# Root-mean-square pooling over four neighbours in fp32 in place: stores in groups of four loads, two of them behind the last load

## The chip, the cores and the metric

The kernel runs on one core of one Trainium2 chip. The metric is the device time of one execution in microseconds (us); lower is better. The core's engines work side by side: ScalarE (ACT in the profile), VectorE (DVE), GpSimd (POOL), SyncE (SP) and TensorE (PE), the last of which is not used here. Transfers between the chip's main memory (HBM) and the core's on-chip memory (SBUF, 128 partitions) are issued from an engine's queue and carried out by 16 DMA engines.

## The reference

The input is 32 x 256 x 4096 numbers in fp32, 134.22 MB. Along the last axis every four neighbours become one number: the square root of the mean of their squares (p is 2, kernel_size is 4). The output is 32 x 256 x 1024 in fp32, 33.55 MB.

```python
for i in range(out_length):                 # out_length = 4096 // 4
    window = np.abs(x[:, :, 4 * i:4 * i + 4]) ** 2.0
    result[:, :, i] = np.mean(window, axis=-1) ** 0.5
```

## The kernel before

The first two axes are flattened to 8192 rows of 4096 numbers. A tile is 256 rows, two consecutive rows for each of the 128 partitions, so that a partition has 8192 numbers (32 KB) and a tile 4 MB; the whole tile is one contiguous stretch of HBM. There are 32 tiles, and one loop over them.

For each tile, the load `xt` (line 50) is issued from SP's queue into one of three input buffers. The tile's arithmetic goes in two halves of 4096 numbers a partition:

- ACT squares the half from `xt` into a tile `x2` in bf16 (line 60);
- DVE adds the first two of every four to the last two, with a `scalar_tensor_tensor` over 2048 pairs, into `c` in bf16 (line 66);
- DVE adds the two numbers that are left, with a second one over 1024, into `sum4` in bf16 (line 73);
- ACT takes the root, with the factor 1/4 as its scale, into half of the output tile `ot` in fp32 (line 78).

When both halves are done, the 1 MB of `ot` are stored by an issue on ACT's queue (line 84). A store's partition holds 8 KB, and there are 32 stores. The tiles `x2`, `c` and `sum4` come from a pool with four buffers each, `ot` from another with four.

The order of the instructions on each engine is set by the framework's scheduler, which also puts in the waits: a load waits until the squares have read the buffer that it is to fill; a square waits for its load, a sum for its square, a root for its sum, and a store for the roots. In the profile, names lose their numbers: `x` stands for `x2` and `sum` for `sum4`.

Of the kernel before, what the change touches and what calls it, by code (L numbers as in the profile page):

```python
# [1 line left out]

# [4 lines left out]


@with_exitstack
def kernel(  # L10
    ctx: ExitStack,
    tc: tile.TileContext,
    x: bass.AP,
    p: float,
    kernel_size: int,
    out: bass.AP,
):
    nc = tc.nc

    assert float(p) == 2.0, "kernel specialized for p == 2"  # L20
    k = int(kernel_size)
    assert k == 4, "kernel specialized for kernel_size == 4"

    x_flat = x.flatten_outer_dims()
    out_flat = out.flatten_outer_dims()
    R, L = x_flat.shape
    P = nc.NUM_PARTITIONS

    ROWS_PER_PART = 2
    CHUNK_ROWS = P * ROWS_PER_PART  # L30
    CL = L * ROWS_PER_PART
    CLo = CL // k
    assert R % CHUNK_ROWS == 0
    n_tiles = R // CHUNK_ROWS
    n_halves = 2
    HL = CL // n_halves
    HLo = HL // k

    fp32 = mybir.dt.float32
    bf16 = mybir.dt.bfloat16  # L40

    in_pool = ctx.enter_context(tc.tile_pool(name="in_pool", bufs=3))
    mid_pool = ctx.enter_context(tc.tile_pool(name="mid_pool", bufs=4))
    out_pool = ctx.enter_context(tc.tile_pool(name="out_pool", bufs=4))

    for i in range(n_tiles):
        rows = slice(i * CHUNK_ROWS, (i + 1) * CHUNK_ROWS)

        xt = in_pool.tile([P, CL], fp32)
        nc.sync.dma_start(  # L50
            out=xt,
            in_=x_flat[rows].rearrange("(p t) l -> p (t l)", t=ROWS_PER_PART),
        )

        ot = out_pool.tile([P, CLo], fp32)
        for h in range(n_halves):
            xh = xt[:, h * HL:(h + 1) * HL]

            x2 = mid_pool.tile([P, HL], bf16)
            nc.scalar.activation(  # L60
                out=x2, in_=xh, func=mybir.ActivationFunctionType.Square,
            )

            x2v = x2.rearrange("p (n j) -> p n j", j=k)
            c = mid_pool.tile([P, 2 * HLo], bf16)
            nc.vector.scalar_tensor_tensor(  # L66
                out=c.rearrange("p (n j) -> p n j", j=2),
                in0=x2v[:, :, 0:2], scalar=1.0, in1=x2v[:, :, 2:4],
                op0=mybir.AluOpType.mult, op1=mybir.AluOpType.add,
            )  # L70
            cv = c.rearrange("p (n j) -> p n j", j=2)
            sum4 = mid_pool.tile([P, HLo], bf16)
            nc.vector.scalar_tensor_tensor(  # L73
                out=sum4, in0=cv[:, :, 0], scalar=1.0, in1=cv[:, :, 1],
                op0=mybir.AluOpType.mult, op1=mybir.AluOpType.add,
            )

            nc.scalar.activation(  # L78
                out=ot[:, h * HLo:(h + 1) * HLo], in_=sum4,
                func=mybir.ActivationFunctionType.Sqrt,  # L80
                scale=1.0 / k,
            )

        nc.scalar.dma_start(
            out=out_flat[rows].rearrange("(p t) l -> p (t l)", t=ROWS_PER_PART),
            in_=ot,
        )


# [1 line left out]
_INS = ['x', 'p', 'kernel_size']  # L91
_OUTS = [((32, 256, 1024), 'float32')]
#: Inputs that are plain numbers.
_NUMBERS = {'p': 2.0, 'kernel_size': 4}


# [26 lines left out]
```

## Time and profile before

| what | value |
|---|---|
| median of 10 runs | 404.67 us (404.61 to 404.8) |
| the profiled execution's own time | 404.62 us |
| its span in the trace | 402.7 us |
| DVE busy | 224.3 us (56%), 128 operations |
| ACT busy | 293.0 us (73%) |
| load queue (q1) | 134.22 MB, 77.5% of the 16 DMA engines' span |
| store queue (q10) | 33.56 MB, 19.8% |
| mean rate over the span | 417 GB/s |

The span is the time from the first to the last event that the trace of the one core holds; the device time has 1.92 us more around it. The trace's page shows busy time of each engine, then the span in 40 slices of about 10 us with busy tenths (9 is 90% or more) and the rate of the DMA engines, then the DMA queues, and the chain of work that ended last. A row of the grouped instructions reads: line, engine, operation, output from input, shapes (partitions x elements, type), count; busy us in total, mean ns of one; idle time of the engine ahead of them, and what ended it. A row of the timeline begins with its start and its duration in us. A row of the windows begins with the stretch, then has its length, the busy time and number of instructions of DVE, ACT and POOL, TensorE's clock, the busy share of the DMA engines and the rate in GB/s. SPq and ACTq are the queues of DMA issues on SP and ACT.

### The profile page before, as it was taken

What the parts mean: (1) busy time and instruction counts of PE and PEld (TensorE: products, weight loads), DVE (VectorE), ACT (ScalarE), POOL (GpSimd) and SP (SyncE); (2) the same over time, 40 slices, a digit from 0 to 9 for tenths busy, and PEclk for the clock granted to TensorE, in tenths of its full rate; (3) what the DMA queues carried; (4) which work ended last, traced back from release to release, by engine and by line L of the source; (5) the groups of instructions that cost most, each with busy time, mean ns of one, the idle gap of its engine ahead of it and who ended that gap; (6) DMA issues with size and microseconds to landing.
All of it is one profiled execution on the core that took longest, in us unless ns stands there. A gap on an engine that the chain in (4) does not pass through costs nothing.

```text
span 402.7 us, 424 instructions
## 1 busy us (share of the span) xinstructions
DVE 224.3 (56%) x128; ACT 293.0 (73%) x130; POOL 0.2 (0%) x4
## 2 busy tenths in 40 slices
DVE  0357466645556554466544566455566554566454
ACT  1788777787676886767977677876767977677872
POOL 0000000000000000000000000000000000000000
DMA  9999999999999999999999999999999999999962
GB/s 361 420 430 403 443 446 404 439 456 404 456 415 431 443 430 426 444 409 448 439 414 445 425 429 448 429 422 444 409 448 427 421 450 425 429 448 404 439 259 104
DMA packets 9219, 167.80 MB, mean 417 GB/s; under 512 B 1024, under 2 KB 1024, under 8 KB 1024
## 3 DMA queue, kind: packets, MB, share of 16 engines
q1 hardware_dynamic: 4608, 134.22, 77.5%
q10 hardware_dynamic: 4608, 33.56, 19.8%
q14 instruction: 3, 0.02, 0.0%
HBM read 134.22 MB, written 33.55 MB: 417 GB/s over the span
## 4 chain that ended last, share of the span: by engine, by line
DMA 58%; ACT 26%; DVE 9%; issue 6%; SPq 0%; ACTq 0%
DMA xt<-in_x_dram 58%; ACT x L60 22%; DVE c L66 6%; ACT ot L78 4%; DVE sum L73 3%; SPq L50 0%; ACTq L78 0%
## 5 line engine op out<-in xcount | busy, mean ns | idle before, releaser
L60 ACT ACTIVATE x<-xt 128x4096 bf16<-128x4096 f32 x64 | 229.1, 3604 | 58.7 <-DMA xt<-in_x_dram 58.7
L66 DVE SCALAR_TENSOR_TENSOR c<-x 128x2048 bf16<-128x2048 bf16 x64 | 146.7, 2292 | 170.4 <-ACT x L60 170.4
L78 ACT ACTIVATE ot<-sum 128x1024 f32<-128x1024 bf16 x64 | 67.1, 1049 | 45.5 <-DVE sum L73 43.8
L73 DVE SCALAR_TENSOR_TENSOR sum<-c 128x1024 bf16<-128x1024 bf16 x64 | 78.4, 1225 | 2.2
L60 ACT ACT_TABLE_LOAD x1 | 1.3, 1283 | 0.7 <-PEq L104 0.7
L78 ACT ACT_TABLE_LOAD x1 | 1.3, 1283 | 0.0
L104 POOL MEMSET const-bfloat16-1.0<- 128x1 bf16 x1 | 0.1, 102 | 0.0
L104 POOL MEMSET const-uint8-127<- 128x1 uint8 x1 | 0.1, 101 | 0.0
L104 POOL MEMSET const-float32-0.0<- 128x1 f32 x1 | 0.1, 99 | 0.2 <-issue 0.2
L104 POOL MEMSET const-float32-1.0<- 128x1 f32 x1 | 0.1, 98 | 0.0
## 6 DMA issues: line engine op xcount, KB each, us to landing
xt<-in_x_dram SPq DMA_DIRECT2D x32, 4096.0 KB, 28.3
out_dram<-ot ACTq DMA_DIRECT2D x32, 1024.0 KB, 16.6
```

What stands on the lines that cost most here:

```text
L60: nc.scalar.activation(out=x2, in_=xh, func=mybir.ActivationFunctionType.Square,)
L66: nc.vector.scalar_tensor_tensor(out=c.rearrange("p (n j) -> p n j", j=2), in0=x2v[:, :, 0:2], scalar=1.0, in1=x2v[:, :, 2:4], op0=mybir.A ...
L73: nc.vector.scalar_tensor_tensor(out=sum4, in0=cv[:, :, 0], scalar=1.0, in1=cv[:, :, 1], op0=mybir.AluOpType.mult, op1=mybir.AluOpType.add,)
L78: nc.scalar.activation(out=ot[:, h * HLo:(h + 1) * HLo], in_=sum4, func=mybir.ActivationFunctionType.Sqrt, scale=1.0 / k,)
L104: nc = _bacc.Bacc("TRN2", target_bir_lowering=False, num_devices=1)
```

## The change

- The layout. The flat input is cut into 32 chunks of 128 x 8192 numbers, and the chunks into groups: seven of four chunks, one of three (chunks 28 to 30) and one of one (chunk 31). Within a group, a partition has one contiguous stretch of HBM, 128 KB in a group of four, and a chunk is a piece of 32 KB of each. So a load still brings 32 KB a partition, but the pieces of neighbouring partitions lie 128 KB apart (96 KB in the group of three, 32 KB in the last).
- The stores. One store a group instead of one a tile: nine in all, of 4 MB (32 KB a partition) for a group of four. Stores of groups 0 to 5 and of the last are issued on ACT's queue after the group's last root. Those of groups 6 and 7 (`held`) are issued on SP's queue after everything else there, that is, behind the last load.
- The arithmetic. Everything is fp32. The square is written over its input in `xt`; one `tensor_reduce` on DVE adds the four neighbours into the group's output tile; the root is taken in place there. The tiles `x2`, `c` and `sum4` are gone.
- The buffers. Four input buffers instead of three, two output buffers of 32 KB a partition, one of 8 KB for the last chunk.
- The order. It is written out by hand (`manual_schedule`). Three loads are issued ahead of the loop and load i+3 at the top of step i; the root of a half is issued on ACT after the square of the next half.
- The first load is issued from ACT's queue, the others from SP's.

The diff, its core:

```diff
-    in_pool = ctx.enter_context(tc.tile_pool(name="in_pool", bufs=3))
-    mid_pool = ctx.enter_context(tc.tile_pool(name="mid_pool", bufs=4))
-    out_pool = ctx.enter_context(tc.tile_pool(name="out_pool", bufs=4))
+    W = 8192
+    CH = 4096
+    GROUP = 4
+    LAST = 1
...
+    while i < n - LAST:
+        g = min(GROUP, n - LAST - i)
+        groups.append((i, g))
+        i += g
+    groups += [(j, 1) for j in range(n - LAST, n)]
+    held = {len(groups) - 1 - LAST - j for j in range(2)}
...
+    in_pool = ctx.enter_context(tc.tile_pool(name="in_pool", bufs=4))
+    out_pool = ctx.enter_context(tc.tile_pool(name="out_pool", bufs=2))
+    last_pool = ctx.enter_context(tc.tile_pool(name="last_pool", bufs=1))
+    ctx.enter_context(tc.manual_schedule())
...
+    def x_block(i):
+        first, g = groups[group_of[i]]
+        block = xf[first * W * P:(first + g) * W * P].rearrange("(p w) -> p w", p=P)
+        return block[:, (i - first) * W:(i - first + 1) * W]
...
+    def load(i):
+        xt = in_pool.tile([P, W], fp32)
+        queue = nc.scalar if i == 0 else nc.sync
+        queue.dma_start(out=xt, in_=x_block(i))
+        xts[i] = xt
+
+    def root(i, c):
+        first, g = groups[group_of[i]]
+        ot = ots[group_of[i]]
+        at = ((i - first) * W + c) // k
+        o = ot[:, at:at + CH // k]
+        nc.scalar.activation(
+            out=o, in_=o, func=mybir.ActivationFunctionType.Sqrt, scale=1.0 / k,
         )
+        if i == first + g - 1 and c + CH == W and group_of[i] not in held:
+            nc.scalar.dma_start(out=out_block(group_of[i]), in_=ot)
...
+    for i in range(3):
+        load(i)
+    pending = None
+    for i in range(n):
+        if i + 3 < n:
+            load(i + 3)
...
+        for c in range(0, W, CH):
+            xh = xts[i][:, c:c + CH]
             nc.scalar.activation(
-                out=x2, in_=xh, func=mybir.ActivationFunctionType.Square,
+                out=xh, in_=xh, func=mybir.ActivationFunctionType.Square,
             )
...
+            nc.vector.tensor_reduce(
+                out=ots[gi][:, at:at + CH // k],
+                in_=xh.rearrange("p (n j) -> p n j", j=k),
+                axis=mybir.AxisListType.X, op=mybir.AluOpType.add,
             )
...
+            if pending is not None:
+                root(*pending)
+            pending = (i, c)
+    root(*pending)
+    for gi in sorted(held):
+        nc.sync.dma_start(out=out_block(gi), in_=ots[gi])
```

More of the change, by code (lines that the diff above doesn't have):

```diff
@@ L22 @@
     assert k == 4, "kernel specialized for kernel_size == 4"
-    x_flat = x.flatten_outer_dims()
-    out_flat = out.flatten_outer_dims()
-    R, L = x_flat.shape
     P = nc.NUM_PARTITIONS
[L29 to L37, printed above, removed]
-    fp32 = mybir.dt.float32
-    bf16 = mybir.dt.bfloat16
-    in_pool = ctx.enter_context(tc.tile_pool(name="in_pool", bufs=3))
@@ L43 @@
-    mid_pool = ctx.enter_context(tc.tile_pool(name="mid_pool", bufs=4))
-    out_pool = ctx.enter_context(tc.tile_pool(name="out_pool", bufs=4))
[L46 to L52, printed above, removed]
-        )
[L55 to L59, printed above, removed]
+    fp32 = mybir.dt.float32
@@ new lines @@
+    xf = x.rearrange("b c l -> (b c l)")
+    of = out.rearrange("b c l -> (b c l)")
+    total = xf.shape[0] // P
+    W = 8192
+    CH = 4096
+    GROUP = 4
+    LAST = 1
+    n = total // W
+    assert n * W == total
+    groups = []
+    i = 0
+    while i < n - LAST:
[4 more added lines that the diff above has]
+    held = {len(groups) - 1 - LAST - j for j in range(2)}
+    group_of = {}
+    for gi, (first, g) in enumerate(groups):
+        for j in range(g):
+            group_of[first + j] = gi
@@ new lines, with out_block @@
+    in_pool = ctx.enter_context(tc.tile_pool(name="in_pool", bufs=4))
[6 more added lines that the diff above has]
+        return block[:, (i - first) * W:(i - first + 1) * W]
+    def out_block(gi):
+        first, g = groups[gi]
+        return of[first * W * P // k:(first + g) * W * P // k].rearrange("(p w) -> p w", p=P)
@@ new lines @@
+    xts = {}
+    ots = {}
+    def load(i):
[10 more added lines that the diff above has]
+            out=o, in_=o, func=mybir.ActivationFunctionType.Sqrt, scale=1.0 / k,
+        )
+        if i == first + g - 1 and c + CH == W and group_of[i] not in held:
+            nc.scalar.dma_start(out=out_block(group_of[i]), in_=ot)
@@ L60 @@
+    for i in range(3):
[4 more added lines that the diff above has]
+            load(i + 3)
+        gi = group_of[i]
+        first, g = groups[gi]
+        if i == first:
+            pool = last_pool if i >= n - LAST else out_pool
+            ot = pool.tile([P, g * W // k], fp32)
+            ots[gi] = ot
+        for c in range(0, W, CH):
+            xh = xts[i][:, c:c + CH]
             nc.scalar.activation(
-                out=x2, in_=xh, func=mybir.ActivationFunctionType.Square,
+                out=xh, in_=xh, func=mybir.ActivationFunctionType.Square,
@@ L62 @@
             )
[L64 to L69, printed above, removed]
-            )
[L71 to L87, printed above, removed]
+            at = ((i - first) * W + c) // k
+            nc.vector.tensor_reduce(
+                out=ots[gi][:, at:at + CH // k],
+                in_=xh.rearrange("p (n j) -> p n j", j=k),
+                axis=mybir.AxisListType.X, op=mybir.AluOpType.add,
+            )
```

## The prediction

> **What bounds the kernel now.** I read the page from the top: busy shares, slices, queues, chain.
>
> ```profile
> span 402.7 us, 424 instructions
> DVE 224.3 (56%) x128; ACT 293.0 (73%) x130; POOL 0.2 (0%) x4
> DMA  9999999999999999999999999999999999999962
> GB/s 361 420 430 403 443 446 404 439 456 404 456 415 431 443 430 426 444 409 448 439 414 445 425 429 448 429 422 444 409 448 427 421 450 425 429 448 404 439 259 104
> ...
> q1 hardware_dynamic: 4608, 134.22, 77.5%
> q10 hardware_dynamic: 4608, 33.56, 19.8%
> ...
> DMA 58%; ACT 26%; DVE 9%; issue 6%; SPq 0%; ACTq 0%
> ```
>
> No compute engine is full; the 16 DMA engines are, in 38 of 40 slices, and loads (q1) and stores (q10) together hold 97.3% of them. The chain that ended last names the DMA for 58% only, because it goes through the squares that free an input buffer; but the transfer rate doesn't sag while it does. So the kernel is bound by bytes, and what can be won lies where the DMA row is not 9: the two ends. The windows view gives these by stretch (engine busy times, clock, DMA share, GB/s):
>
> ```profile
> 5.00:385.00 380.00, 217.12 (x124) 281.58 (x124) 0.00 (x0) 1.00 1.00 431
> 0.00:1.60 1.60, 0.00 (x0) 0.88 (x1) 0.20 (x4) 1.00 0.00 0
> ...
> 385.00:390.00 5.00, 0.37 (x2) 4.74 (x3) 0.00 (x0) 1.00 0.78 321
> 390.00:398.50 8.50, 6.84 (x4) 5.44 (x3) 0.00 (x0) 1.00 0.00 1
> 398.50:402.70 4.20, 0.00 (x0) 0.00 (x0) 0.00 (x0) 1.00 0.61 250
> ...
> 401.40:401.80 0.40, 0.00 (x0) 0.00 (x0) 0.00 (x0) 1.00 0.02 0
> ```
>
> For 380 us the share is 1.00 at 431 GB/s. At the end the DMA stands still for over 8.5 us, and the timeline shows what it waits for: the last tile's arithmetic.
>
> ```profile
> 386.22 3.60 ACT L60 ACTIVATE x<-xt 128x4096 bf16<-128x4096 f32 x1
> 386.34 0.34 ACTq L84 DMA_DIRECT2D out_dram<-ot  x1
> 389.73 3.60 ACT L60 ACTIVATE x<-xt 128x4096 bf16<-128x4096 f32 x1
> ...
> 393.36 2.29 DVE L66 SCALAR_TENSOR_TENSOR c<-x 128x2048 bf16<-128x2048 bf16 x1
> ...
> 395.68 1.23 DVE L73 SCALAR_TENSOR_TENSOR sum<-c 128x1024 bf16<-128x1024 bf16 x1
> 396.94 1.06 ACT L78 ACTIVATE ot<-sum 128x1024 f32<-128x1024 bf16 x1 [2.45 <-DVE sum L73]
> 398.03 0.34 ACTq L84 DMA_DIRECT2D out_dram<-ot  x1
> ```
>
> Squares, sums and root of tile 31 run with nothing left to move; only then is its 1 MB stored.
>
> **The change, part by part.**
>
> *Held stores (the main term).* The stores of chunks 24-27 (4 MB) and 28-30 (3 MB) go onto SP's queue behind load 31. Their bytes are not new; they are moved from beside the loads to behind the last one: 7.34 MB at 431 GB/s, 17.0 us of transfer that covers the last chunk's arithmetic. Nothing is queued behind them on SP, and load 31 stands ahead of them, so no load waits for a root. What becomes free is the standstill: 0.22 x 5.00 = 1.1 us in 385-390, 8.5 us in 390-398.5, and in the last 4.2 us a 0.39 share, 1.6 us, less the 1.3 us from 401.4 to 402.7 that any last store has. Together 9.9 us; some of the 1.1 us is only the 16 engines ending unevenly, so I take 9.6, with 9.0 and 9.9 as ends.
>
> Whether the cover holds is a race, priced with these rows:
>
> ```profile
> L60 ACT ACTIVATE x<-xt 128x4096 bf16<-128x4096 f32 x64 | 229.1, 3604 | 58.7 <-DMA xt<-in_x_dram 58.7
> L66 DVE SCALAR_TENSOR_TENSOR c<-x 128x2048 bf16<-128x2048 bf16 x64 | 146.7, 2292 | 170.4 <-ACT x L60 170.4
> L78 ACT ACTIVATE ot<-sum 128x1024 f32<-128x1024 bf16 x64 | 67.1, 1049 | 45.5 <-DVE sum L73 43.8
> L73 DVE SCALAR_TENSOR_TENSOR sum<-c 128x1024 bf16<-128x1024 bf16 x64 | 78.4, 1225 | 2.2
> ```
>
> and, for the time from the last store's issue (398.03) to its bytes, the windows
>
> ```profile
> 398.40:398.80 0.40, 0.00 (x0) 0.00 (x0) 0.00 (x0) 1.00 0.00 0
> 398.80:399.20 0.40, 0.00 (x0) 0.00 (x0) 0.00 (x0) 1.00 0.98 410
> ```
>
> The new sum over four has no row. The two DVE rows give (2292-1225)/1024 = 1.04 ns a position and 158 ns fixed. A reduction that takes one input a cycle has 4096 positions: 4.43 us. If it took two inputs a cycle, as the two-operand sums do, 2.29 us; at half speed for 4-byte data, 158 + 8536 = 8.7 us. I take 4.43: nothing in the rows shows a penalty for 4-byte data (the square reads it and the root writes it: the difference of their means, 2555 ns over 3072 elements, is one 0.83 ns slope for both). By the same token square and root in fp32 stay 3.60 and 1.05.
>
> From the end of load 31's bytes, with 1.6 us until ACT sees it (an estimate, as long as from the span's start to the first packets): square 0 ends at 5.2, the held-back root of chunk 30 at 6.2, so SP, which waits for just that root, issues store 28-30 with its first bytes some 0.8 us later (398.03 to 398.80 above), at 7.0. Store 24-27, long released, lasts till 9.7: 2.7 us of slack. Square 1 ends at 9.7, reduction 0 at 9.6, reduction 1 at 14.1, the last root at 15.2, its store's bytes start at 16.0. The held stores end at 17.0: 1.0 us of slack. The last MB then ends with the rest and the 1.3 us closing follows.
>
> *Compute between the loads.*
>
> ```profile
> 360.98 1.06 ACT L78 ACTIVATE ot<-sum 128x1024 f32<-128x1024 bf16 x1 [2.67 <-DVE sum L73]
> 361.94 3.60 ACT L60 ACTIVATE x<-xt 128x4096 bf16<-128x4096 f32 x1
> ...
> 365.45 3.60 ACT L60 ACTIVATE x<-xt 128x4096 bf16<-128x4096 f32 x1
> ```
>
> By the distances of these starts a half costs ACT 3.51 for the square (361.94 to 365.45) and 0.96 for the root, 4.47 us; DVE 4.43 plus a handover of 0.03. A chunk takes 8.9 us. A load alone takes 4.19 MB / 431 = 9.7 us, and on average with its store 12.2. So compute keeps up even in stretches with loads only, by 0.8 us a chunk: no cost, the DMA covers it. If that cover went, each us a chunk beyond 9.7 delays the last six chunks first. DVE rises from 225 to 283 us, ACT stays near 297, both under 390. Four input buffers instead of three: a chunk's buffer is free some 14 us after it lands, while two to three loads are still queued, so no load starts late.
>
> *Fewer, longer stores.* 33.56 MB cost 19.8% of 402.7 = 79.7 us in 8 KB pieces a partition; at the loads' price (77.5% for 134.22 MB, 312.1 us) they would cost 78.0. The gain is up to 1.7 us. Against it: a store alone is seen once, 1.05 MB from 398.8 to 401.4, at 403 GB/s; if all 8.39 MB of the new tail ran so, they would lose 1.4 us. I take -1.5, since that lone MB holds the start and uneven end that only the last store will have.
>
> Mid-run stores will share the engines evenly with the loads. The issues by line (KB each, us to landing):
>
> ```profile
> xt<-in_x_dram SPq DMA_DIRECT2D x32, 4096.0 KB, 28.3
> out_dram<-ot ACTq DMA_DIRECT2D x32, 1024.0 KB, 16.6
> ```
>
> and the timeline's start shows what the first load moves past:
>
> ```profile
> 0.72 1.28 ACT L60 ACT_TABLE_LOAD   x1 [0.72 <-PEq L104]
> 0.73 19.64 SPq L50 DMA_DIRECT2D xt<-in_x_dram  x4
> 12.90 7.12 ACT L60 ACTIVATE x<-xt 128x4096 bf16<-128x4096 f32 x2 [10.89 <-DMA xt<-in_x_dram]
> ```
>
> 1 MB takes 16.6 us to land beside loads, far over its own 2.6, so queues alternate; with equal pieces a 4 MB store takes about 19.5 us and a load beside it twice 9.7. A group comes every 49 us and has two output buffers, so no reduction waits for a store. The 0.34 us issue on ACT falls from 32 to 7; hidden.
>
> *First load on ACT's queue.* It then shares the engines with load 1 and both land near 21 us instead of the first at 12.9. Compute starts 8-9 us later, which the 3.3 us a chunk (12.2 less 8.9) wins back; the DMA is busy with four queued loads (39 us). Cost 0; ends -0.4 (one SP issue saved) and +1.3 (the table load goes first and holds it back).
>
> **Sum**, against the profiled execution, 404.62 us = span 402.7 + 1.92 around it (median of ten runs 404.67, so nothing to correct): -9.6 - 1.5, and +0.5 for unevenness at three new queue hand-overs (a guess, between 0 and the 1.1 us that the present end shows): 394.0 us.
>
> **Rivals.** (B) *The cover tears.* The slack of 1.0 us is thin. If reductions take 4.9 us or more a half, compute falls behind 9.7 us loads by 0.1 us a chunk and up, over six chunks, and the last root comes after the held stores; likewise if landing takes longer. Each us late is a us of standstill, at most the 9.6. Middle: 398.
>
> (C) *Loads run slower in the new layout.* A partition's row is now 128 KB from the next one instead of 32 KB. Each per cent off the loads is 3.1 us; from 10.6 / 312.1 = 3.4% on the change loses. Priced by the page's slices: the slow ones near 404 GB/s against 431 would make the loads 332 us, +20, thus 414. For it: no row shows such a distance; against: 8 KB and 32 KB distances now run within 2% of one another.
> The Trainium skill, page "DMA: Bandwidth & Descriptors", section "Latency and other measured facts", says that large power-of-two distances between partitions' rows in HBM slow copies: 207 GB/s at 512 KiB against 214 at full rate, far less at megabytes. Taken at 128 KB that 3.3% would be 10.3 us, by estimate 404, no change; no trace here shows it, and a quarter of that distance should cost less.
>
> (D) *Slower: the halves wait for one another.* Square 1 now writes the very tile that reduction 0 reads, and root and reduction share one output tile. If the waits go by whole tile, a half runs in series: 3.60 + 4.43 + 1.05 = 9.1 us, 64 of them 581 us, plus ends about 600. It decides when a half exceeds 6.1 us (12.2 a chunk). Before shows no such sharing between engines; the slices written are disjoint, which speaks against it.
>
> (E) *The reduction at half speed:* 64 x 8.7 = 556, with first load and tail some 580 us. Slower than before from about 5.6 us a half on. Against: the slopes above.
>
> **How the numbers follow.** A (as summed) 0.76, B 0.12, C 0.05, D 0.04, E 0.03. A's terms at their good ends together give 392.6 (9.9, 1.7 and 0.4 off, the hand-overs at nothing), at their bad ends 399.4 (9.0 off, 1.4, 1.3 and 1.1 on); that range takes in most of B as well and leaves out some 0.15. Ten runs lie within 0.05%; I take 0.2%, 0.8 us, as what can be told from no change. Faster: A and B, 0.88. Within: the part of C with 3.2 to 3.7% off the loads and its near surroundings, 0.02. Slower: the rest of C, D and E, 0.10.
>
> **What would show it.** Right: reductions near 4.43 us; DMA share 1.00 up to 2 us before the end; three last store issues (SP, SP, ACT) whose bytes join without a gap; first square near 21 us. Wrong: a hole in the DMA row after the last load (B); q1 per byte dearer (C); squares waiting for the DVE (D, E).

## The result, and the profile after

The changed kernel takes 395.46 us (median of 8 runs, 395.25 to 395.60) against 404.68 us before: a ratio of 0.9771, 95% interval 0.9762 to 0.9779. The forecast was 394.0 us with a range of 392.6 to 399.4; its span would have been 392.1 us, and is 393.4. In all comparisons below, the kernel before ran on the same chip beside the others, at 404.61 to 404.68 us.

From the page of the changed kernel: span, busy shares, DMA slices, queues, and the two groups whose duration was forecast.

```profile
span 393.4 us, 357 instructions
DVE 282.8 (72%) x64; ACT 294.0 (75%) x130; POOL 0.2 (0%) x4
DMA  8999999999999999999999999999999999999997
...
q1 hardware_dynamic: 4752, 137.37, 81.3%
q10 hardware_dynamic: 1152, 30.41, 18.0%
...
L113 DVE TENSOR_REDUCE ot<-xt 128x1024 f32<-128x4096 f32 x64 | 282.8, 4419 | 103.1 <-ACT xt L109 102.3
L109 ACT ACTIVATE xt<-xt 128x4096 f32<-128x4096 f32 x64 | 230.8, 3608 | 87.5 <-DMA xt<-in_x_dram 85.0
```

The last two slices, 6 and 2 before, are 9 and 7. DVE works 58 us more than before and nothing becomes longer by it. The tail, by the windows (stretch, busy times, clock, DMA share, GB/s) and by the timeline:

```profile
5.00:385.00 380.00, 281.90 (x64) 291.68 (x128) 0.00 (x0) 1.00 1.00 431
385.00:390.00 5.00, 0.86 (x1) 1.06 (x1) 0.00 (x0) 1.00 0.97 372
390.00:393.40 3.40, 0.00 (x0) 0.00 (x0) 0.00 (x0) 1.00 0.46 195
```

```profile
363.63 3.62 ACT L109 ACTIVATE xt<-xt 128x4096 f32<-128x4096 f32 x1 [0.55 <-DMA xt<-in_x_dram]
...
373.34 3.62 ACT L109 ACTIVATE xt<-xt 128x4096 f32<-128x4096 f32 x1 [0.54 <-DMA xt<-in_x_dram]
...
377.93 0.34 SPq L123 DMA_DIRECT2D out_dram<-ot  x1
...
385.89 1.06 ACT L88 ACTIVATE ot<-ot 128x1024 f32<-128x1024 f32 x1 [3.39 <-DVE ot L113]
386.98 0.34 ACTq L92 DMA_DIRECT2D out_dram<-ot  x1
```

The middle runs at the same 431 GB/s as before. In 385-390 the DMA now stands still for 0.03 x 5.00 = 0.15 us and in the last 3.4 us for 0.54 x 3.40 = 1.8 us. The same sum over the tail before was 1.1 + 8.5 + 1.6 = 11.2 us. So 9.2 us of standstill went, and the span fell by 402.7 - 393.4 = 9.3 us: all of the gain lies in the tail. While the last chunk is worked, the 7 MB behind load 31 move. (The 372 GB/s in 385-390 do not mean a hole: a window counts a transfer with all its bytes where it starts, so that the long pieces under way at 385 are counted ahead of it.) The timeline's first two rows show the pace: chunks 30 and 31 begin 9.71 us apart, and each time ACT has waited about half a microsecond for the load, so compute is not behind.

Whether the held stores alone do this, and what the rest of the change is worth, the page can't tell. Twelve more kernels were run for it.

### The profile page after: what moved, and what is told of

It is laid out like the page before. It is cut to its first block, busy times and chain, and to the rows that moved or that the text cites. A ratio compares the mean times of both kernels' runs of the same rounds, so it can differ in the third digit from the quotient of the medians.

```text
span 393.4 us, 357 instructions
## 1 busy us (share of the span) xinstructions
DVE 282.8 (72%) x64; ACT 294.0 (75%) x130; POOL 0.2 (0%) x4
## 4 chain that ended last, share of the span: by engine, by line
DMA 65%; ACT 21%; DVE 11%; issue 0%; ACTq 0%
DMA xt<-in_x_dram 65%; ACT xt L109 18%; DVE ot L113 11%; ACT ot L88 3%; ACT L88 0%; ACTq L109 0%
## 5 line engine op out<-in xcount | busy, mean ns | idle before, releaser
L113 DVE TENSOR_REDUCE ot<-xt 128x1024 f32<-128x4096 f32 x64 | 282.8, 4419 | 103.1 <-ACT xt L109 102.3
L109 ACT ACTIVATE xt<-xt 128x4096 f32<-128x4096 f32 x64 | 230.8, 3608 | 87.5 <-DMA xt<-in_x_dram 85.0
L88 ACT ACTIVATE ot<-ot 128x1024 f32<-128x1024 f32 x64 | 67.0, 1047 | 4.2 <-DVE ot L113 3.4
```

Of the source, the lines that this page charges most:

```text
L88: nc.scalar.activation(out=o, in_=o, func=mybir.ActivationFunctionType.Sqrt, scale=1.0 / k,)
L109: nc.scalar.activation(out=xh, in_=xh, func=mybir.ActivationFunctionType.Square,)
L113: nc.vector.tensor_reduce(out=ots[gi][:, at:at + CH // k], in_=xh.rearrange("p (n j) -> p n j", j=k), axis=mybir.AxisListType.X, op=mybir. ...
```

## Experiments

**1. The changed kernel with nothing held.**

```diff
-    held = {len(groups) - 1 - LAST - j for j in range(2)}
+    held = set()
```

> The changed kernel with every store issued on ACT's queue after its group's last root, none held behind the last load. Theory (the held stores fill the standstill of the tail): the 4 MB of chunks 24-27 go back beside the loads, load 31 lands 9.7 us later, and only the 3 MB of chunks 28-30 and the last 1 MB are left behind it. Their bytes start about 7 us after the last load's bytes end, so a hole of some 7 us opens, a second of 1 to 2 us after them, and the time is 403.9 us (402.5 to 405). Rival (the gain comes from longer stores, the fp32 arithmetic or the order): 395.5 to 397.

Measured: 403.58 us (403.30 to 404.05), ratio 0.9972 (0.9962 to 0.9982). The windows of the tail:

```profile
380.00:385.00 5.00, 4.97 (x2) 4.43 (x3) 0.00 (x0) 1.00 0.26 111
385.00:390.00 5.00, 4.18 (x2) 4.58 (x3) 0.00 (x0) 1.00 0.37 157
390.00:395.00 5.00, 4.44 (x2) 2.66 (x2) 0.00 (x0) 1.00 0.97 418
395.00:402.00 7.00, 1.17 (x1) 1.06 (x1) 0.00 (x0) 1.00 0.46 188
```

Between 380 and 390 the DMA stands still for 3.7 + 3.2 = 6.9 us, then come the 3 MB and, after a second hole, the last one. Without the held stores 8.1 of the 9.2 us are gone. Where the remaining 1.1 us come from was not taken apart.

**2. The kernel before with the seven stores ahead of its last one held.**

```diff
-    mid_pool = ctx.enter_context(tc.tile_pool(name="mid_pool", bufs=4))
-    out_pool = ctx.enter_context(tc.tile_pool(name="out_pool", bufs=4))
+    mid_pool = ctx.enter_context(tc.tile_pool(name="mid_pool", bufs=2))
+    out_pool = ctx.enter_context(tc.tile_pool(name="out_pool", bufs=8))
...
-        nc.scalar.dma_start(
...
+        if n_tiles - 8 <= i < n_tiles - 1:
+            kept.append((to, ot))
+        else:
+            nc.scalar.dma_start(out=to, in_=ot)
+    for to, ot in kept:
+        nc.sync.dma_start(out=to, in_=ot)
```

> The kernel before with one thing changed: the stores of tiles 24 to 30 (seven of 1 MB) are issued on SP's queue behind the last load; eight output buffers instead of four, and two buffers instead of four for the bf16 tiles to make room. Theory (held stores alone carry the gain): 7.34 MB, 17 us, cover the last tile's 12 us of arithmetic; 404.68 less 8.8 is 395.9 us (395.2 to 397). Rival (the gain needs the fp32 arithmetic, the hand-written order or the longer stores): 400 to 405.

Measured: 402.40 us (402.36 to 402.44), ratio 0.9943 (0.9929 to 0.9956). The theory as it stood is wrong: this edit brings 2.3 us, not 8.8. The timeline of ACT shows why (the squares and roots are one line further down than in the kernel before):

```profile
371.03 1.06 ACT L79 ACTIVATE ot<-sum 128x1024 f32<-128x1024 bf16 x1 [2.45 <-DVE sum L74]
371.99 7.11 ACT L61 ACTIVATE x<-xt 128x4096 bf16<-128x4096 f32 x2
379.21 1.06 ACT L79 ACTIVATE ot<-sum 128x1024 f32<-128x1024 bf16 x1
382.71 1.06 ACT L79 ACTIVATE ot<-sum 128x1024 f32<-128x1024 bf16 x1 [2.45 <-DVE sum L74]
383.68 7.11 ACT L61 ACTIVATE x<-xt 128x4096 bf16<-128x4096 f32 x2
...
394.40 1.06 ACT L79 ACTIVATE ot<-sum 128x1024 f32<-128x1024 bf16 x1 [2.45 <-DVE sum L74]
395.49 0.34 ACTq L89 DMA_DIRECT2D out_dram<-ot  x1
```

```profile
385.00:390.00 5.00, 2.66 (x2) 5.00 (x2) 0.00 (x0) 1.00 0.80 338
390.00:395.00 5.00, 4.33 (x3) 2.44 (x3) 0.00 (x0) 1.00 0.00 0
395.00:400.60 5.60, 0.00 (x0) 0.46 (x1) 0.00 (x0) 1.00 0.45 187
```

From tile 25 on, both squares of a tile run first, then both of its roots, and the second root waits 2.45 us for its sums with the next tile's squares behind it. A tile begins every 383.68 - 371.99 = 11.69 us. That would be enough where a load comes with its store (12.2 us), but with the stores held a load alone takes 9.7 us. ACT falls 2 us further behind at each tile, and waits for no load any more. The last root ends at 395.5, when the held stores have long run out: 5.0 us of hole in 390-395 and 1.0 us before.

This is not quite the order of the kernel before. There, and in this run up to tile 24, the scheduler puts the second root of every other tile behind the next tile's first square, so that only one tile in two waits for its sums. The kernel before, between the squares of tile 29 (361.94 and 365.45, shown in the prediction) and those of tile 31 (386.22):

```profile
369.16 1.06 ACT L78 ACTIVATE ot<-sum 128x1024 f32<-128x1024 bf16 x1
373.57 3.62 ACT L60 ACTIVATE x<-xt 128x4096 bf16<-128x4096 f32 x1 [3.36 <-DMA xt<-in_x_dram]
377.09 1.04 ACT L78 ACTIVATE ot<-sum 128x1024 f32<-128x1024 bf16 x1
378.04 3.60 ACT L60 ACTIVATE x<-xt 128x4096 bf16<-128x4096 f32 x1
...
381.55 1.04 ACT L78 ACTIVATE ot<-sum 128x1024 f32<-128x1024 bf16 x1
385.26 1.06 ACT L78 ACTIVATE ot<-sum 128x1024 f32<-128x1024 bf16 x1 [2.67 <-DVE sum L73]
```

Two tiles take 24.28 us here, of which 3.36 us are a wait for a load; without that wait a tile costs ACT 10.46 us. This too is below the 12.2 us of a load with its store and above the 9.7 us of a load alone. So the edit of experiment 2 changed more than the place of the stores: with them held, the scheduler chose a slower order for the last seven tiles. (The other buffer counts cost nothing up to there: tile 24 begins at 300.91 us, and at 300.76 in the kernel before.) What held stores would bring in the order before, no run shows; by the same count, an estimate, ACT would fall behind by 0.8 us a tile instead of 2.0.

From here the theory is: the two parts pay only together. The held stores make a stretch with loads only, and the order of the root decides whether compute can follow it.

**3. Experiment 2 with the order of the changed kernel.** Arithmetic in bf16 with two sums, 1 MB stores and the layout stay as before. The core of the edit:

```diff
+    ctx.enter_context(tc.manual_schedule())
...
-            nc.scalar.activation(out=ot[...], in_=sum4, func=Sqrt, ...)
+            if pending is not None:
+                root(*pending)          # the root of the half before
+            pending = (i, h, ot, sum4)
```

> The kernel before with held stores (402.4 us) and one thing more: the order of the changed kernel. It is written out by hand, with each half's root on ACT behind the next half's square; the arithmetic stays bf16 with two sums, the stores stay 1 MB, the layout as before. Theory (held stores pay only where compute runs faster than the 9.7 us of a load alone; before, ACT waits 2.5 us a tile for the sums and needs 11.7 us a tile, so it ends late behind the last seven loads): a tile now takes 2 x 4.47 = 8.9 us and the time is 395.6 us (395.2 to 396.2). Rival (the single fp32 reduction is what makes the tail short): 399 to 402.4.

Measured: 395.57 us (395.42 to 395.63), ratio 0.9775 (0.9760 to 0.9789): the time of the changed kernel, without its arithmetic, its layout or its long stores. The 11.7 us a tile that the theory calls the pace before is that of experiment 2; in the kernel before it is 10.5. ACT's rows, with the wait for the load back in the brackets:

```profile
363.28 3.62 ACT L83 ACTIVATE x<-xt 128x4096 bf16<-128x4096 f32 x1 [0.69 <-DMA xt<-in_x_dram]
...
366.80 1.04 ACT L60 ACTIVATE ot<-sum 128x1024 f32<-128x1024 bf16 x1
...
373.00 3.62 ACT L83 ACTIVATE x<-xt 128x4096 bf16<-128x4096 f32 x1 [0.70 <-DMA xt<-in_x_dram]
```

**4. The order alone.** Experiment 3 with every store issued on ACT after its own root, none held.

> The kernel before with the hand-written order (root behind the next half's square) and no held stores: bf16_order with every 1 MB store issued after its own root. Theory (order and held stores pay only together: with loads and stores side by side a tile's bytes take 12.2 us, and the pace before of 11.7 is enough): the last load lands as before, the last tile takes about as long, 404.5 us (404.0 to 404.9), no change. Rival (the order pays by itself): 402.5 or less.

Measured: 405.29 us (405.04 to 405.39), ratio 1.0016 (1.0006 to 1.0025). The order by itself brings nothing, rather a loss of 0.7 us. In the last tile, the second root of tile 30 and the issue of its store now stand between the two squares:

```profile
385.50 3.62 ACT L80 ACTIVATE x<-xt 128x4096 bf16<-128x4096 f32 x1 [2.60 <-DMA xt<-in_x_dram]
389.02 1.04 ACT L60 ACTIVATE ot<-sum 128x1024 f32<-128x1024 bf16 x1
...
390.09 0.34 ACTq L68 DMA_DIRECT2D out_dram<-ot  x1
390.48 3.62 ACT L80 ACTIVATE x<-xt 128x4096 bf16<-128x4096 f32 x1 [0.41 <-ACT ot L60]
```

The first square starts 0.72 us earlier than before (386.22), the second 4.98 us behind it instead of 3.51, and the last issue comes at 398.80 instead of 398.03. With experiments 2 to 4 the table of two by two is full: neither 404.6, held only 402.4, order only 405.3, both 395.6. Two things limit it: "held only" has the scheduler's other order in its last seven tiles, and "neither" has other buffer counts than the rest (4 and 4 for the bf16 and output tiles, against 2 and 8).

**5. The changed kernel with both squares of a chunk first, then both roots.** This is the order of the last seven tiles of experiment 2; the kernel before has it in every other tile only.

```diff
         for c in range(0, W, CH):   # both squares, both reductions
-            if pending is not None:
-                root(*pending)
-            pending = (i, c)
+        for c in range(0, W, CH):
+            root(i, c)
```

> The changed kernel with the order of the one before: both squares of a chunk first, then both roots. Theory (the pace of a chunk is set by what ACT waits for): the second root waits for both reductions, 3.6 + 2 x 4.43 + 1.06 = 13.5 us a chunk, above the 12.2 us of a chunk's bytes; 22.7 + 32 x 13.5 + the last store's 5.6 + 1.9 = 462 us (455 to 468), slower than the kernel before. Rival (DMA stays the bound and only the tail suffers): 396 to 405.

Measured: 460.70 us (460.65 to 460.81), ratio 1.1385 (1.1368 to 1.1402).

```profile
198.32 7.11 ACT L108 ACTIVATE xt<-xt 128x4096 f32<-128x4096 f32 x2
...
210.73 1.06 ACT L88 ACTIVATE ot<-ot 128x1024 f32<-128x1024 f32 x1 [3.27 <-DVE ot L112]
211.69 7.11 ACT L108 ACTIVATE xt<-xt 128x4096 f32<-128x4096 f32 x2
```

A chunk every 13.37 us, above the 12.2 us of its bytes. So the single fp32 reduction, 4.42 us against 2.29 + 1.23 before, is no help here: with it in this order the kernel is 56 us slower than the one before, and the new order hides it.

**6. One more reduction ahead of the very last.**

```diff
+            if i == n - 1 and c + CH == W:
+                nc.vector.tensor_reduce(out=scratch, in_=<the same half>, ...)
             nc.vector.tensor_reduce(
```

> The changed kernel with one more reduction of 4.42 us (over the same 4096 numbers, into a scratch tile that nobody reads) on DVE ahead of the very last one. Theory (the held stores cover the last chunk with about 1 us to spare): the last store's bytes start 4.4 us later, the rest of the slack is used up and the remainder shows, 398.5 us (397.9 to 399.3), with a hole in the DMA row before the last MB. Rivals: (cover much longer than thought) 395.5; (no slack at all) 399.9 or more.

Measured: 398.00 us (397.80 to 398.15). The last store's issue moved from 386.98 to 391.23, by 4.25 us, and 2.5 us of it show in the time:

```profile
388.00:389.00 1.00, 1.00 (x1) 0.00 (x0) 0.00 (x0) 1.00 0.18 74
389.00:390.00 1.00, 1.00 (x1) 0.00 (x0) 0.00 (x0) 1.00 0.00 0
390.00:391.00 1.00, 0.11 (x1) 0.85 (x1) 0.00 (x0) 1.00 0.00 0
391.00:392.00 1.00, 0.00 (x0) 0.20 (x1) 0.00 (x0) 1.00 0.00 0
```

The rows make the hole look longer than 2.5 us, since the held stores' last pieces start before 389 and run on. The cover has 1.7 us to spare, where the prediction had 1.0.

**7. Groups of one: loads contiguous, stores of 1 MB with 8 KB a partition; the same seven held.**

```diff
-    GROUP = 4
+    GROUP = 1
...
-    held = {len(groups) - 1 - LAST - j for j in range(2)}
+    held = {len(groups) - 1 - LAST - j for j in range(7)}
...
-    out_pool = ctx.enter_context(tc.tile_pool(name="out_pool", bufs=2))
+    out_pool = ctx.enter_context(tc.tile_pool(name="out_pool", bufs=8))
```

> The changed kernel with groups of one chunk: every load is one contiguous 4 MB stretch again (partitions 32 KB apart), every store 1 MB with 8 KB a partition; the seven stores before the last are held, the same bytes as now. Theory (longer stores save their pieces' cost, the loads' distance of 128 KB costs nothing): 33.5 MB of stores at the old price, about 1 us more: 396.5 us (396.0 to 397.2). Rival (rows 128 KB apart slow the loads): the loads gain back what they lost, 395.3 or less.

Measured: 395.50 us (395.44 to 395.86), ratio 0.9775 (0.9761 to 0.9788). Neither forecast: no 1 us more, and no gain either. Where stores run alone, the longer pieces are indeed faster, as the same stretch of the two kernels shows (the changed kernel first, then this one):

```profile
374.00:387.00 13.00, 10.99 (x3) 9.52 (x5) 0.00 (x0) 1.00 1.02 440
```

```profile
374.00:387.00 13.00, 10.64 (x3) 9.18 (x5) 0.00 (x0) 1.00 1.01 426
```

As a window counts a piece where it starts, the share has to be set against the rate: 440 / 1.02 = 431 against 426 / 1.01 = 422, some 2% of the 17 us of held stores, 0.3 us. Chunk 31 begins earlier by about as much with short pieces (373.00 there, 373.34 in the changed kernel), so the stretch before takes it back.

The single transfers that the two traces hold show how. A store's piece of 8 KB takes 309 ns, one of 32 KB 1213 ns instead of 4 x 309 = 1236, beside loads as well as alone. All stores together take 79.1 us of the 16 engines' time with short pieces and 78.2 with long ones: 0.9 us less. But the loads take 312.4 us in the changed kernel and 311.5 here: a 32 KB piece of a load takes 1220 ns on average there, and 1217 here. From 5 to 50 us, ahead of the first store, the changed kernel's load pieces take 1213 ns, so their distance of 128 KB alone does not do it. They became dearer from the first store on, most of all while it began (65 to 70 us). Why the long stores do more of this than the short ones, no run shows.

**8. Groups of two: pieces 64 KB apart for loads, 16 KB a partition for stores.**

> The changed kernel with groups of two chunks: loads with pieces 64 KB apart, stores of 2 MB in 16 KB pieces, the seven MB before the last held. Theory (longer store pieces save about 1 us, the wider distance of the loads costs about 1 us, so groups of four and of one come out alike): in between, 395.0 to 395.5 us; 395.0 if the distance costs nothing yet at 64 KB. Rival (neither matters): 395.5.

Measured: 395.45 us (395.27 to 395.49), ratio 0.9773 (0.9758 to 0.9788), as with groups of one and four. In the time of this kernel the length of a store's piece is worth nothing measurable from 8 to 32 KB. That the stores gain and the loads lose about as much, as the theory had it, is borne out here too (78.3 us for the stores, 312.4 for the loads); that the distance of the loads is the reason is not.

**9. Pieces 1 MB apart.** The whole input is one group for the addresses of loads and stores; the pieces of a store then lie 256 KB apart.

```diff
-        block = xf[first * W * P:(first + g) * W * P].rearrange("(p w) -> p w", p=P)
-        return block[:, (i - first) * W:(i - first + 1) * W]
+        block = xf.rearrange("(p w) -> p w", p=P)
+        return block[:, i * W:(i + 1) * W]
...
-        return of[first * W * P // k:(first + g) * W * P // k].rearrange("(p w) -> p w", p=P)
+        block = of.rearrange("(p w) -> p w", p=P)
+        return block[:, first * W // k:(first + g) * W // k]
```

> The changed kernel with the whole input as one group for the addresses: a partition owns 1 MB of the input, so each load takes 32 KB pieces 1 MB apart, and each store 32 KB pieces 256 KB apart. Theory of the prediction's rival C, as the packets of the load-only stretches hint (1213 ns a 32 KB piece at 32 KB distance, 1220 at 128 KB): the distance costs little at 128 KB but grows; by the Trainium skill's page on DMA (DMA: Bandwidth & Descriptors, Latency and other measured facts), between 207 of 214 GB/s at 512 KiB and 164 of 214 at 2 MiB, 3 to 23%. From the rows alone: if the 0.6% goes with the distance, 8 times that is 5% of 312 us, +15, 410 us (400 to 470). Rival (distance doesn't matter, the 7 ns have another cause): 395.5.

Measured: 405.68 us (403.29 to 406.11), 10 us over the changed kernel, and a ratio of 1.0014 (0.9994 to 1.0034) to the one before. But the rate is not lower throughout:

```profile
5.00:20.00 15.00, 0.00 (x0) 0.00 (x0) 0.00 (x0) 1.00 1.00 345
20.00:50.00 30.00, 17.30 (x4) 21.55 (x9) 0.00 (x0) 1.00 0.99 380
50.00:385.00 335.00, 255.84 (x59) 262.57 (x117) 0.00 (x0) 1.00 1.00 429
350.00:370.00 20.00, 18.19 (x5) 18.76 (x9) 0.00 (x0) 1.00 1.00 433
```

The changed kernel has 437 GB/s in 5-20 and 431 over 5-385. Here the first 50 us are slow and the rest hardly is, with the same distances. The Trainium skill, page "DMA: Bandwidth & Descriptors", section "Latency and other measured facts", gives 207 GB/s at 512 KiB and 164 at 2 MiB against 214 at full rate, for copies from HBM to HBM with rows of 16 KiB. The trace agrees that a wide distance costs, but for the most part only until some 50 us into the run; why it stops then no run here shows.

**10. The first load on SP's queue.**

```diff
-        queue = nc.scalar if i == 0 else nc.sync
+        queue = nc.sync
```

> The changed kernel with load 0 on SP's queue like the others. Theory (the first load's queue is worth nothing, since the DMA engines are full either way and compute has slack): 395.5 us, within 0.4; the first square starts near 13 us instead of 22.7. Rival (the second queue saves the issue or the ramp): 0.4 to 1 us slower; or (compute has too little slack after the late start): faster by up to 1 us.

Measured: 395.54 us (395.47 to 395.72), ratio 0.9774 (0.9760 to 0.9787). The first square starts at 12.86 us instead of 22.70, and the time is the same.

**11. The last chunk in four pieces.**

```diff
-        for c in range(0, W, CH):
+        h = CH if i < n - 1 else CH // 2
+        for c in range(0, W, h):
...
```

> The changed kernel with the last chunk worked in four pieces of 2048 instead of two of 4096. The last root then ends some 1.8 us earlier, and the last MB joins the held stores while they still run. Theory (the DMA ran below its rate for about 1 us where the held stores end and the last one starts up): 395.0 us (394.7 to 395.3). Rival (bytes alone set the end, the start-up costs nothing): 395.5.

Measured: 395.44 us (395.37 to 395.61): no change, but the edit missed its aim. The last store was issued at 386.99, as before (386.98): DVE is busy with chunk 30 until about 376.3 either way, ACT waited 0.93 us for it with the held-back root of that chunk, and afterwards has a root behind each of four squares. What an earlier last store would bring stays open. The changed kernel's own trace says how little stands still where the held stores end: the DMA shares of the six microseconds from 385 to 391 are 1.03, 1.14, 1.03, 0.92, 0.72 and 0.95, 0.97 on average, 0.2 us.

**12. Only the store of chunks 24-27 held.**

```diff
-    held = {len(groups) - 1 - LAST - j for j in range(2)}
+    held = {len(groups) - 2 - LAST}
```

> The changed kernel with only the store of chunks 24-27 held behind the last load; that of chunks 28-30 goes on ACT's queue after its last root. Theory (that root comes after the first square of chunk 31 anyway, so its store's bytes can't start before the 4 MB in front have nearly ended, whichever queue it is on): 395.5 us, within 0.4. Rival (both must be in one queue in front of the last store): 396 to 398, as the ACT issue holds up the last chunk or the queues end unevenly.

Measured: 395.08 us (394.95 to 395.26), ratio 0.9764 (0.9748 to 0.9780). One held store of 4 MB is enough: the store of chunks 28-30 was issued at 377.95 on ACT, at 377.93 on SP in the changed kernel. It is the fastest of all kernels here, but its interval overlaps that of the changed kernel, so the 0.4 us are not shown to be a gain. In its trace the last store's 128 pieces of 8 KB take 309 ns each, in that of the changed kernel 370, which is 0.5 us over 16 engines; one trace of each does not show whether that is the rule.

## Why the prediction was right, and where it was not

- *The bound and the place of the gain:* right. The middle kept its 431 GB/s, and the tail gave 9.2 us where 9.6 less 0.5 were forecast.
- *The race in the tail:* right to a tenth. From the start of square 0 of chunk 31, the forecast had the last root ending after 15.2 - 1.6 = 13.6 us; it ended at 386.95, 13.6 us after 373.34. The held root and the store behind it came as worked out (4.6 us to the issue). The slack was 1.7 us (experiment 6), not 1.0, on the safe side of rival B.
- *The reduction at one input a cycle:* right, 4419 ns against 4.43 us; square and root kept 3608 and 1047 ns in fp32 and in place. Rivals D and E fall. In the page, DVE waits for ACT, and ACT waits 3.4 us for DVE in all: halves of one tile do not hold one another up. The argument against E from square and root was weak, though: two rows always give one slope.
- *Longer stores, -1.5 us:* the mis-sized term. Experiments 7 and 8 put it at 0.0 to 0.1 us in the time, which is as much as lies between 394.0 and 395.46. The stores' own share of the 16 engines' time did fall, by 0.9 us from experiment 7 to the changed kernel, where the prediction had up to 1.7. What the sum put at nothing is the other side: the loads of the kernel with longer stores took 0.8 us more.
- *The hand-overs, +0.5 us:* a guess, and no run measures it by itself. The trace has 0.2 us of standstill where the held stores end. That the held stores and the guess together come out at 9.1 us, against 9.2 measured, may be partly luck.
- *Compute between the loads, at no cost:* the sum was right, but it was put down as a condition and its other side not drawn. The pace of 8.9 us a chunk was compared with the loads, while the pace before was never worked out from its rows: 10.5 us a tile in the order of the kernel before, above the 9.7 us of a load alone. The prediction therefore called the held stores the main term. In truth they brought 2.3 us in experiment 2, where the scheduler's order gave 11.7 us a tile, and 8.1 (experiment 1) to 9.7 us (experiment 4 against 3) with the new order. The expectation for experiment 2 carried that fault.
- *The first load:* right, nothing (experiment 10).
- *Rival C:* at 128 KB no loss shows in the pace: chunks come 9.71 us apart with pieces 128 KB apart (363.63 to 373.34) and 9.72 us with pieces 32 KB apart (363.28 to 373.00, experiment 3). The 3 ns by which a load's piece is dearer on average set in only with the first store (experiment 7). That the distance can cost is shown, at 1 MB.

## What to carry to other kernels

When a kernel is bound by its transfers, the tail in which the last tile is worked with nothing left to move can be filled with stores kept back for it. Kept-back stores leave a stretch in which loads come faster, so work out the pace of compute against a load alone, not against load and store together: an engine that waits for another in the middle of a tile may have just enough pace for the one and not for the other. Two edits that are each worth little or nothing (2.3 us and -0.7 us here) can be worth 9 together, so test all four combinations, and look in each trace whether the scheduler kept the order of instructions that the comparison assumes.

## What the runs showed of the hardware

Transfers whose pieces lie 1 MB apart ran at 345 GB/s at first and at 433 GB/s later in the same run, with no change in the program. A piece of 8 KB took 309 ns and one of 32 KB 1213 ns, so that short pieces cost 2% more a byte, beside another queue as well as alone (experiment 7). Longer stores made the kernel no faster all the same, since a load's piece of 32 KB then took 1220 ns on average instead of 1217; the cause of that is open.
